# PSUM banks of attention and of the streams beside it: one shared pool of four, or three and one

## The chip, the core and the metric

The kernel runs on one core of a Trainium2 chip. The time is the device time of one execution in microseconds (us), here the median of three runs; beside it stands one execution that the hardware profiler recorded, from which all lines of the profile come. The engines are named as the profile names them: PE is TensorE (its matrix products; PEld its weight loads), DVE is VectorE, ACT is ScalarE, POOL is GpSimd, SP is SyncE, which issues most DMAs. TensorE writes its results into PSUM, which this kernel uses as eight banks of 128 partitions by 512 fp32 numbers.

## What is computed

One decoder block on 2048 tokens of width 1024, in fp32. A modulation of the conditioning vector gives shifts, scales and gates. Then, cut to what matters here:

```
h    = RMSNorm(x) * (1 + scale) + shift
proj = h W_in  ->  q_a, k_a, v_a | q_m, k_m, v_m, o_m, i_m, f_m | g_a, g_m
y_a  = sliding-window attention of rope(q_a), rope(k_a), v_a:  8 query heads, 2 key/value heads,
       16 blocks of 128 queries against 256 keys, a learned sink per head in the softmax
y_m  = chunkwise mLSTM of silu(conv4(q_m, k_m)), v_m and the gates i_m, f_m, with a layer norm
       per head and an output gate
mix  = (sigmoid(g_a) (y_a W_A) + sigmoid(g_m) (y_m W_B)) W_out
x    = x + gate * RMSNorm(mix);   then the same sandwich around a SwiGLU FFN of width 2816
```

## The kernel before

**Stages.** The 2048 tokens are worked in two superblocks of 1024, each of two blocks of 512 (four tiles of 128 tokens). `superblock` gives the order for one of them: queries and keys/values of the first block, `attend(b0)`, mLSTM values of that block, keys/values and queries of the second block, the first quarter of its mLSTM values, `attend(b1)`, the rest of them, then fourteen pairs of wide feature tiles (mLSTM queries, keys, output gate, branch gates), and at last the branch products and `W_out` of both blocks. The FFN follows for both superblocks. A large product is split into a high and a low fp32r part of each operand, so it is three products in PSUM (`mm3`); its sums stand in the four banks of the pool `ps_acc` (tile name `acc`), its split weights in `whi` and `wlo` (L266, L267).

**Small work beside large work.** Attention, gates, rotary steps, h of the next block (`hprep`) and mLSTM are written as generators, "streams". `spawn` registers one, `tick` steps those that are due between the products of the large work, by a planned time `now` that counts TensorE's products; each `yield` gives the planned delay to its next step. So the order in which the code asks for tiles is the order of these planned steps. The final order of instructions on each engine is set when the kernel is built, by a scheduler with a timing model of its own, which can move an instruction ahead of others that wait for a tile or for data.

**The shared banks.** The other four PSUM banks are the pool `ps_mix`. All short users take their bank from it by `mix_tile` (L120), under one tag with four buffers (tile name `mix`):

- `one` in `hprep` (L496): four transposes of x; ScalarE reads the bank twice (L502, L504). Eight such tiles for a block of h.
- `q_stream` (L756) and `k_stream` (L783): transposes of the rotated queries and keys of one token tile (`mix<-ident,tx`), read by ScalarE and VectorE (L763, L764; L789, L790), then stored to `at_d`, from where attention loads them as `at`.
- `gates` (L824): two tiles for a block.
- `attention` (L899): for a block of 128 queries four tiles of scores in two halves (`mix<-at`, read by L927 on ScalarE and L929 on VectorE), after the softmax (L934 to L946, its last step on POOL) two tiles of transposed probabilities (`mix<-ident,tm`, read by L955 and L959), and one of the output (`mix<-tm,at`, read by L968 and L973). Two `attention_stream`s alternate; behind L968 each issues the load of its next block on ScalarE's queue (L896).
- `chunk_state` (L1010) and `chunk_out` (L1051) of mLSTM: seven tiles for a chunk, with `vmt`, `ld` and `cst` as operands.
- `ada_tail` (L404), and in the later stages `h_combine`, `pair_parts` for the FFN and the `Y` sums of `down`.

**Scratch.** `tx` (L123) is a pool of nine tiles of 512 columns in SBUF. `evac_q` (L770) empties a query bank of `acc` into one (L773), and `rope` takes a second; both are held until `q_stream` has stored its result. `evac_kv` (L795, L798) and `k_stream` hold two in the same way. `rope` ends with L752 and L753 on VectorE. In between, `attend(b)` (L998) first finishes the query and key streams of its block, then lets attention go on, and spawns the two attention streams once in a superblock.

Of the kernel before, what the change touches and what calls it, by code (L numbers as in the profile page):

```python
# [10 lines left out]
F32 = mybir.dt.float32  # L11
# [8 lines left out]
P = 128  # L20
# [4 lines left out]
NT = TB // P  # L25
# [47 lines left out]
def decoder_block(ctx: ExitStack, tc: tile.TileContext, a: dict, out: bass.AP, dbg=None):  # L73
# [32 lines left out]
    ps_mix = ctx.enter_context(tc.tile_pool(name="ps_mix", bufs=4, space=PSUM))  # L106
# [6 lines left out]
    def nm(s):  # L113
        uid[0] += 1
        return f"{s}{uid[0]}"

    def acc_tile():
        return ps_acc.tile([P, 512], F32, tag="acc", name=nm("acc"))

    def mix_tile():  # L120
        return ps_mix.tile([P, 512], F32, tag="mix", name=nm("mix"))

    def tx(shape, dtype=F32):  # L123
        return tpool.tile(shape, dtype, tag="tx", name=nm("tx"), bufs=9)
# [1 line left out]
    def tm(shape, dtype=F32):  # L126
        return mpool.tile(shape, dtype, tag="tm", name=nm("tm"), bufs=9)
# [79 lines left out]
    def mm(o, lhsT, rhs, start, stop, resumed=False):  # L207

        n = int(np.prod(rhs.shape[1:]))
        now[0] += max(110.0, n * 0.422) if rhs.dtype == F32R else max(218.0, n * 1.7)  # L210
        T.matmul(o, lhsT=lhsT, rhs=rhs, start=start, stop=stop, skip_group_check=resumed)  # L211

    def transpose(o, i):
        now[0] += 110.0
        k = i.shape[0]
        T.transpose(o, i, ident[:k, :k])  # L216

    def spawn(gen, delay=0.0):
        st = [now[0] + delay, gen, False]
        streams.append(st)  # L220
        return st
# [506 lines left out]
    def superblock(sb):  # L728
# [170 lines left out]
        def attention(n, a_, ahead):  # L899
            first = n == 0  # L900
            b, t = divmod(n, NT)
            k0 = P if first else 0
            ks = slice(k0, 2 * P)
            af = a_.bitcast(F32)
            later = None
            qth, qtl = (a_[:, i * 512:(i + 1) * 512].rearrange("p (j q) -> p j q", j=GQ) for i in range(2))
            kth, ktl = (a_[:, AT_K + 2 * i * P:AT_K + 2 * (i + 1) * P] for i in range(2))
            vat = af[:, AT_V:].rearrange("p (u d) -> p u d", u=2)
            mx = small.tile([P, HQ], F32, tag="mx", name=nm("mx"))
            nm_ = small.tile([P, HQ], F32, tag="nmx", name=nm("nmx"))  # L910
            sums = small.tile([P, HQ], F32, tag="sums", name=nm("sums"))
            es = small.tile([P, HQ], F32, tag="es", name=nm("es"))
            banks = {}
            sc = {g: tm([P, GQ, P]) for g in range(2)}
            for jj in range(2):
                for g in range(2):
                    banks[g, jj] = mix_tile()
                for u in range(2):
                    j = 2 * jj + u
                    for lt, rt, st_, sp_ in ((qth, kth, True, False), (qth, ktl, False, False), (qtl, kth, False, True)):  # L920
                        for g in range(2):
                            pr = slice(g * 64, (g + 1) * 64)
                            mm(banks[g, jj][:, u * 256 + k0:u * 256 + 256], lt[pr, j, :], rt[pr, ks], st_, sp_)
                for g in range(2):
                    bv = banks[g, jj].rearrange("p (u k) -> p u k", u=2)
                    dst = sc[g][:, 2 * jj:2 * jj + 2, :]
                    A.copy(dst, bv[:, :, P:])  # L927
                    mk = m_prev.bitcast(U32).unsqueeze(1).to_broadcast([P, 2, P])
                    V.copy_predicated(dst, mk, negc.unsqueeze(1).to_broadcast([P, 2, P]) if first else bv[:, :, :P])  # L929
                if jj == 0:  # L930
                    yield 0
            for g in range(2):
                hs = slice(g * GQ, (g + 1) * GQ)
                V.tensor_reduce(mx[:, hs], sc[g], axis=AX.X, op=ALU.max)  # L934
            V.tensor_tensor(mx, mx, sinks, op=ALU.max)
            V.tensor_scalar(nm_, mx, -1.0, None, op0=ALU.mult)
            V.tensor_tensor(es, sinks, mx, op=ALU.subtract)
            A.activation(es, es, AF.Exp)
            for g in range(2):
                for j in range(GQ):  # L940
                    hd = g * GQ + j
                    A.activation(sc[g][:, j, :], sc[g][:, j, :], AF.Exp, bias=nm_[:, hd:hd + 1], accum_out=sums[:, hd:hd + 1])
                hs = slice(g * GQ, (g + 1) * GQ)
                V.tensor_tensor(sums[:, hs], sums[:, hs], es[:, hs], op=ALU.add)
                V.reciprocal(sums[:, hs], sums[:, hs])
                G.tensor_tensor(sc[g], sc[g], sums[:, hs].unsqueeze(2).to_broadcast([P, GQ, P]), op=ALU.mult)  # L946
            yield L_SOFT
            pcs, pfs = [], []
            for g in range(2):
                pt = mix_tile()  # L950
                for j in range(GQ):
                    transpose(pt[:, j * P:(j + 1) * P], sc[g][:, j, :])
                pf = tm([P, GQ, P])
                ptv = pt.rearrange("p (j q) -> p j q", j=GQ)
                A.copy(pf, ptv)  # L955
                pfs.append(pf)
                if not first:
                    pc = tm([P, GQ, P])
                    V.scalar_tensor_tensor(pc, cneg.unsqueeze(1).to_broadcast([P, GQ, P]), -1.0, ptv, op0=ALU.is_ge, op1=ALU.mult)  # L959
                    pcs.append(pc)  # L960
                yield L_PT if g == 0 else L_PV
            yps = mix_tile()
            for src_, u, st_, sp_ in ((pfs, int(first), True, first), (pcs, 1, False, True)):
                for g, p_ in enumerate(src_):
                    mm(yps[g * 64:(g + 1) * 64, :], vat[:, u, g * 64:(g + 1) * 64], p_.rearrange("p j q -> p (j q)"), st_, sp_)
            now[0] -= 1500.0
            yh, yl = tm([P, 512], F32R), tm([P, 512], F32R)
            A.copy(yh, yps)  # L968
            y_out = [y_d[b][:, i, :, t * P:(t + 1) * P] for i in range(2)]
            nc.scalar.dma_start(y_out[0], yh.bitcast(F32).rearrange("p (j q) -> p j q", j=GQ))  # L970
            if ahead():
                later = load_at(n + 2, nc.scalar)
            V.tensor_tensor(yl, yps, yh.bitcast(F32), op=ALU.subtract)  # L973
            yield 700.0
            nc.scalar.dma_start(y_out[1], yl.bitcast(F32).rearrange("p (j q) -> p j q", j=GQ))
            return later
# [3 lines left out]
        def attention_stream(u):  # L980
            a_ = None
            for i in range(u, 2 * NT, 2):
                n = b0 * NT + i
                if a_ is None:
                    while i >= ready[0]:
                        yield 1000.0
                    a_ = load_at(n, nc.sync)
                    yield L_LOAD
                    a_ = yield from attention(n, a_, lambda: i + 2 < ready[0])
                else:  # L990
                    yield L_LOAD - 1500.0
                    a_ = yield from attention(n, a_, lambda: i + 2 < ready[0])
                done_att[0] += 1
                yield 500.0

        done_att = [0]

        def attend(b):  # L998
            finish(R["qk"])
            ready[0] = (b - b0 + 1) * NT  # L1000
            if b == b0:
                R["att"] = [spawn(attention_stream(0), L_QK), spawn(attention_stream(1), L_QK + L_ATT2)]
            R["gs", b] = [spawn(gates(b), L_QK)]

# [5 lines left out]
        def chunk_state(c):  # L1010
            b, t = b0 + c // NT, c % NT
# [9 lines left out]
            vc = vmt[n_ % 2]  # L1021
            nc.sync.dma_start(vc[:, :, :MD], vm_d[b][:, t, :].rearrange("p (h d) -> p h d", h=MH))
            yield L_LOAD
            pk = mix_tile()
            for hh in range(MH):
                transpose(pk[:, hh * P:(hh + 1) * P], km[:, hh, :])
            kw = tm([P, MH, P])
# [10 lines left out]
                G.tensor_tensor(qs_, qs_, qm, op=ALU.mult)  # L1038
            R["w", c] = wd, qs_, km, qm, vc
            yield L_KW  # L1040
            pcn = [mix_tile() for _ in range(2)]
            for hh in range(MH):
                mm(pcn[hh // 2][:, (hh % 2) * 129:(hh % 2) * 129 + 129], kw[:, hh, :], vc[:, hh, :], True, True)
            for hh in range(MH):
# [6 lines left out]
        def chunk_out(c):  # L1051
            b, t = b0 + c // NT, c % NT
# [1 line left out]
            cs = slice(t * P, (t + 1) * P)  # L1054
            n_ = b * NT + t
            wd, qs_, km, qm, vc = R["w", c]
            pS = mix_tile()
            for hh in range(MH):
                mm(pS[:, hh * P:(hh + 1) * P], km[:, hh, :], qm[:, hh, :], True, True)
            V.tensor_tensor(wd, pS.rearrange("p (h t) -> p h t", h=MH), wd, op=ALU.mult)  # L1060
# [4 lines left out]
            st = small.tile([P, MH, 6], F32, tag="st", name=nm("st"))  # L1065
            mv = small.tile([P, MH, 2], F32, tag="mv", name=nm("mv"))
            vr = small.tile([P, MH], F32, tag="vr", name=nm("vr"))
            pn = [mix_tile() for _ in range(2)]
            for hh in range(MH):
                o = pn[hh // 2][:, (hh % 2) * 129:(hh % 2) * 129 + 129]  # L1070
                if n_ > 0:
# [20 lines left out]
                o = pn[hh // 2][:, (hh % 2) * 129:(hh % 2) * 129 + P]  # L1092
                A.activation(ym[:, hh, :], o, AF.Identity, scale=cf[:, hh:hh + 1], bias=vr[:, hh:hh + 1])
            yield L_LN
            py = mix_tile()
            for hh in range(MH):
                transpose(py[:, hh * P:(hh + 1) * P], ym[:, hh, :])
            V.tensor_tensor(om, py.rearrange("p (h t) -> p h t", h=MH), om, op=ALU.mult)
# [1019 lines left out]
```

## Time and profile before

| what | value |
|---|---|
| median of 3 runs | 2687.98 us (2685.71 to 2688.53) |
| profiled execution, its own time | 2687.54 us |
| its span, first to last instruction | 2685.5 us |
| mean granted TensorE clock | 0.993 |
| PE busy | 2629.6 us (98%), 12382 products |
| DVE busy | 1988.3 us (74%) |
| ACT busy | 1298.8 us (48%) |
| POOL busy | 140.4 us (5%) |
| DMA moved | 511.89 MB |

Busy time counts an engine's instructions without those that only wait or issue DMAs; products are pipelined, so a busy PE isn't always a PE at its best pitch. In the timelines a row gives the start, the length, the engine, the line of the kernel, the operation, the tiles `out<-in` with their buffer numbers left out, shapes and a count, and in brackets the idle time of that engine just ahead with what ended it. In the windows a row gives a stretch, its length, the busy time of each engine with a count, the granted clock, the DMA engines' share and GB/s.

### The profile page before, as it was taken

What the parts mean: (1) busy time and instruction counts of PE and PEld (TensorE: products, weight loads), DVE (VectorE), ACT (ScalarE), POOL (GpSimd) and SP (SyncE); (2) the same over time, 40 slices, a digit from 0 to 9 for tenths busy, and PEclk for the clock granted to TensorE, in tenths of its full rate; (3) what the DMA queues carried; (4) which work ended last, traced back from release to release, by engine and by line L of the source; (5) the groups of instructions that cost most, each with busy time, mean ns of one, the idle gap of its engine ahead of it and who ended that gap; (6) DMA issues with size and microseconds to landing.
All of it is one profiled execution on the core that took longest, in us unless ns stands there. A gap on an engine that the chain in (4) does not pass through costs nothing.

```text
span 2685.5 us, 35800 instructions
## 1 busy us (share of the span) xinstructions
PE 2629.6 (98%) x12382; PEld 2146.8 (80%) x12382; DVE 1988.3 (74%) x3882; ACT 1298.8 (48%) x2525; POOL 140.4 (5%) x181
## 2 busy tenths in 40 slices
PE   7899999999998999999999999999999999999998
PEld 6777788888886778888877888888777888888886
DVE  7888887768696988876677777775677676666466
ACT  4656544545754654444654343335554333333444
POOL 0100001200101000110000000000000000000000
PEclk9999999999999999999999999999999999999999
DMA  7564456897575644678775555446675232334566
GB/s 252 173 231 144 148 175 185 263 345 246 191 245 160 210 141 151 194 239 321 227 243 176 181 180 180 134 143 219 214 247 188 98 114 97 108 99 148 189 204 219
DMA packets 353637, 511.89 MB, mean 191 GB/s; under 512 B 25120, under 2 KB 213660, under 8 KB 348208
## 3 DMA queue, kind: packets, MB, share of 16 engines
q1 hardware_dynamic: 335240, 493.82, 55.4%
q10 hardware_dynamic: 18216, 15.79, 2.0%
q8 instruction: 97, 1.59, 0.2%
q14 instruction: 84, 0.69, 0.1%
HBM read 357.12 MB, written 144.02 MB: 187 GB/s over the span
## 4 chain that ended last, share of the span: by engine, by line
PE 63%; DVE 3%; DMA 1%; ACT 1%; issue 0%; POOL 0%; SPq 0%; DVEq 0%; POOLq 0%; ACTq 0%
PE acc L211 42%; PE mix L211 20%; DVE hl L1608 1%; PE mix L216 1%; DMA raw<-as_d 1%; ACT hl L1607 1%; DMA raw<-ws_d 0%; DMA raw<-in_w_ffn_down_dram 0%; DVE big L1608 0%; DVE w L1918 0%; DVE big L1931 0%; DVE w L1954 0%; DVE w L1959 0%; ACT big L1653 0%; POOL rs L457 0%
## 5 line engine op out<-in xcount | busy, mean ns | idle before, releaser
L211 PE MATMUL acc<-big,hl 128*128 128x512 f32 x3936 | 933.9, 392 | 1.4 <-ACT hl L1607 0.7
L211 PEld LDWEIGHTS acc<-big,hl 128*128 128x128 f32 x3936 | 732.9, 188 | 164.8 <-issue 10.0
L1607 ACT CAST hl<-raw 128x512 fp32r<-128x512 f32 x732 | 440.7, 621 | 504.7 <-PE acc L211 238.7
L1608 DVE TENSOR_TENSOR hl<-raw,hl 128x512 fp32r<-128x512 f32 x732 | 497.5, 695 | 190.1 <-ACT hl L1607 187.8
L211 PE MATMUL acc<-whi,big 128*128 128x512 f32 (+1 forms) x1216 | 356.7, 374 | 7.9 <-ACT tx L89 3.8
L211 PE MATMUL mix<-big,hl 128*128 128x512 f32 x1056 | 263.0, 390 | 1.7 <-ACT hl L1607 1.0
L211 PEld LDWEIGHTS acc<-whi,big 128*128 128x128 f32 x1216 | 222.1, 191 | 50.9 <-ACT tx L89 4.3
L211 PE MATMUL acc<-hl,hl 128*128 128x512 f32 x1008 | 238.8, 395 | 5.8 <-DVE hl L1608 3.4
L211 PEld LDWEIGHTS mix<-big,hl 128*128 128x128 f32 x1056 | 197.7, 188 | 44.5 <-ACT hl L1607 1.9
L211 PEld LDWEIGHTS acc<-hl,hl 128*128 128x128 f32 x1008 | 188.0, 189 | 52.1 <-DVE hl L1608 8.4
L211 PE MATMUL acc<-wlo,big 128*128 128x512 f32 (+1 forms) x608 | 226.0, 374 | 3.0 <-DVE wlo L267 3.0
L211 PE MATMUL mix<-hl,hl 128*128 128x512 f32 x792 | 182.6, 391 | 1.1 <-DVE hl L1608 0.9
L211 PEld LDWEIGHTS mix<-hl,hl 128*128 128x128 f32 x792 | 147.9, 188 | 34.8 <-DVE hl L1608 3.0
L211 PE MATMUL acc<-big,whi 128*128 128x512 f32 x512 | 158.2, 393 | 0.0
L267 DVE TENSOR_TENSOR wlo<-raw,whi 128x1024 fp32r<-128x1024 f32 (+1 forms) x95 | 109.8, 1156 | 64.6 <-ACT whi L266 58.4
L266 ACT CAST whi<-raw 128x1024 fp32r<-128x1024 f32 (+1 forms) x95 | 93.7, 987 | 112.5 <-PE acc L211 102.5
L211 PEld LDWEIGHTS acc<-wlo,big 128*128 128x128 f32 x608 | 115.6, 190 | 24.0 <-DVE wlo L267 4.6
L457 POOL TENSOR_TENSOR rs<-ms,halves 128x1 f32<-128x1 f32 (+1 forms) x56 | 43.6, 791 | 1647.1 <-DVE ms L455 1637.5
L211 PE MATMUL mix<-hcT4h,hl 128*128 128x512 f32 x352 | 115.6, 389 | 0.7 <-ACT hl L1607 0.7
L211 PE MATMUL acc<-hcT2h,hl 128*128 128x512 f32 x352 | 115.5, 389 | 0.0
L211 PEld LDWEIGHTS acc<-big,whi 128*128 128x128 f32 x512 | 95.4, 188 | 19.6 <-DMA big<-y_d 0.4
L211 PE MATMUL acc<-big,wlo 128*128 128x512 f32 x256 | 97.6, 392 | 0.0
(350 smaller groups left out, 3537.2 us busy)
## 6 DMA issues: line engine op xcount, KB each, us to landing
raw<-in_w_in_dram SPq DMA_DIRECT2D x48, 1024.0 KB, 6.7
as_d<-w SPq DMA_DIRECT2D x154, 256.0 KB, 2.1
raw<-as_d SPq DMA_DIRECT2D x70, 512.0 KB, 3.9
raw<-in_w_ffn_gate_dram SPq DMA_DIRECT2D x22, 1024.0 KB, 5.5
raw<-in_w_ffn_up_dram SPq DMA_DIRECT2D x22, 1024.0 KB, 6.0
raw<-ws_d SPq DMA_DIRECT2D x40, 512.0 KB, 4.6
tx<-in_w_ada_dram SPq DMA_DIRECT2D x64, 256.0 KB, 3.7
g_d<-tx SPq DMA_DIRECT2D x64, 256.0 KB, 2.5
```

The lines of the kernel that those rows point to most:

```text
L211: T.matmul(o, lhsT=lhsT, rhs=rhs, start=start, stop=stop, skip_group_check=resumed)
L216: T.transpose(o, i, ident[:k, :k])
L266: A.copy(hv, src)
L267: V.tensor_tensor(lv, src, hv.bitcast(F32), op=ALU.subtract)
L457: G.tensor_tensor(r[:, :n], ms[:, :n], nhalf[:, :n], op=ALU.pow)
L1607: A.copy(v(hi), src)
L1608: V.tensor_tensor(v(lo), src, v(hi).bitcast(F32), op=ALU.subtract)
```

## The change

The pool's one tag `mix` with four buffers becomes two tags: `mixa` with three and `mixb` with one. The list `attending` is filled in `attend` of a superblock's first block, behind the finish of its query and key streams, and cleared when its eight attention blocks have been stepped through. `att_tile` is always `mixa`. `mix_tile` is `mixb` while `attending` holds something; otherwise it takes `mixa` three times and `mixb` the fourth. `wide_tile` is `mixa` while attention is under way and `mix_tile` otherwise. Attention uses `att_tile`, mLSTM `wide_tile`, all others keep `mix_tile`. No arithmetic and no transfer is changed.

```
+    N_ATT = 3
+    turn, attending = [0], []
+
+    def att_tile():
+        return ps_mix.tile([P, 512], F32, tag="mixa", name=nm("mix"), bufs=N_ATT)
+
     def mix_tile():
-        return ps_mix.tile([P, 512], F32, tag="mix", name=nm("mix"))
+        if not attending:
+            turn[0] += 1
+            if turn[0] % 4 :
+                return att_tile()
+        return ps_mix.tile([P, 512], F32, tag="mixb", name=nm("mix"), bufs=4 - N_ATT)
+
+    def wide_tile():
+        return att_tile() if attending else mix_tile()
...
@@ attention @@
-                    banks[g, jj] = mix_tile()
+                    banks[g, jj] = att_tile()
...
-                pt = mix_tile()
+                pt = att_tile()
...
-            yps = mix_tile()
+            yps = att_tile()
...
                 done_att[0] += 1
+                if done_att[0] == 2 * NT:
+                    attending.clear()
...
             if b == b0:
+                attending.append(b)
...
@@ chunk_state; in the same way pcn, and pS, pn, py of chunk_out @@
-            pk = mix_tile()
+            pk = wide_tile()
```

More of the change, by code (lines that the diff above doesn't have):

```diff
@@ L1040, in chunk_state @@
             yield L_KW
-            pcn = [mix_tile() for _ in range(2)]
+            pcn = [wide_tile() for _ in range(2)]
             for hh in range(MH):
@@ L1056, in chunk_out @@
             wd, qs_, km, qm, vc = R["w", c]
-            pS = mix_tile()
+            pS = wide_tile()
             for hh in range(MH):
@@ L1067, in chunk_out @@
             vr = small.tile([P, MH], F32, tag="vr", name=nm("vr"))
-            pn = [mix_tile() for _ in range(2)]
+            pn = [wide_tile() for _ in range(2)]
             for hh in range(MH):
@@ L1094, in chunk_out @@
             yield L_LN
-            py = mix_tile()
+            py = wide_tile()
             for hh in range(MH):
```

## The prediction

> **What bounds the kernel now.** I read the page first, then the chain that ended last, then the stages in windows, then the timelines of the two weak stages.
>
> ```profile
> PE 2629.6 (98%) x12382; PEld 2146.8 (80%) x12382; DVE 1988.3 (74%) x3882; ACT 1298.8 (48%) x2525; POOL 140.4 (5%) x181
> ...
> PE 63%; DVE 3%; DMA 1%; ACT 1%; issue 0%; POOL 0%; SPq 0%; DVEq 0%; POOLq 0%; ACTq 0%
> ```
>
> ```profile
> 1656.09 5.44 PE acc L211 x24
> ```
>
> TensorE is the bound: 98% busy and nearly all of the chain. Fed without a break it runs 24 wide products in 5.44 us, 227 ns each. No bank layout changes that pitch; a change of banks can only remove or add stretches in which TensorE isn't fed. So I looked for such stretches while attention runs, since outside them the change only renames the same four banks (below). The windows of all engines give two, one for each superblock:
>
> ```profile
> 117.00:132.00 15.00, 10.19 (x50) 6.82 (x49) 11.07 (x29) 12.88 (x42) 4.12 (x4) 0.89 0.26 67
> 794.00:813.00 19.00, 18.71 (x95) 15.73 (x94) 18.39 (x73) 15.19 (x51) 6.07 (x4) 1.00 0.50 162
> ...
> 832.00:857.00 25.00, 17.55 (x74) 9.29 (x73) 13.43 (x38) 14.81 (x52) 4.69 (x5) 0.80 0.38 119
> 857.00:877.00 20.00, 20.00 (x110) 16.54 (x109) 19.13 (x44) 8.49 (x15) 0.00 (x0) 1.00 0.80 265
> ```
>
> The columns are the stretch, its length, busy time of PE, PEld, DVE, ACT, POOL, and then the granted clock. In 832:857 TensorE is idle for 25.00 - 17.55 = 7.45 us and its clock is 0.80; in 117:132 it is idle for 4.81 us at 0.89; right behind, 857:877, nothing is lost. The timeline of PE tells what it ran and waited for in the first:
>
> ```profile
> 831.44 0.97 PE L211 MATMUL mix<-at 64*128 64x256 f32 x6
> 836.68 2.93 PE L211 MATMUL mix<-at 64*128 64x256 f32 x24 [4.26 <-DVE sums L945]
> 841.05 3.31 PE L211 MATMUL mix<-tm,at 128*64 128x512 f32 x8 [0.24 <-ACT tm L955]
> 846.88 1.12 PE L216 MATMUL mix<-ident,tm 128*128 128x128 f32 x4 [2.53 <-POOL tm L946]
> 848.41 1.12 PE L216 MATMUL mix<-ident,tm 128*128 128x128 f32 x4 [0.41 <-POOL tm L946]
> 851.36 0.69 PE L216 MATMUL mix<-ident,tx 128*128 128x128 f32 x2
> 854.72 0.48 PE L211 MATMUL acc<-whi,big 128*128 128x512 f32 x1
> ```
>
> Attention's own waits (4.26 + 0.24 + 2.53 + 0.41 = 7.44 us) are the idle time. They hurt because no projection product (`acc`) runs before 854.72. Why not? The 4.26 us also shows how far planned order and chip differ: the row names DVE L945, but the keys and queries for this block were requested at 828.23, and such a load lands 6.0 to 8.3 us later (836.5 at the latest), so I read it as the load.
>
> ```profile
> 816.46 0.59 ACT L773 COPY tx<-acc 128x512 f32<-128x512 f32 x1 [0.31 <-PE acc L211]
> ...
> 828.23 0.34 ACTq L896 DMA_DIRECT2D at<-at_d  x1
> ...
> 852.25 0.59 ACT L773 COPY tx<-acc 128x512 f32<-128x512 f32 x1
> ```
>
> ```profile
> DMA to landing us min/median/max: 6.0/7.2/8.3
> ```
>
> L773 empties a query bank of `acc` into a `tx` tile. The first of this block is at 816.46, the second at 852.25, just behind the key transposes of 851.36. There are nine `tx` tiles. Each of four `k_stream`s holds two from L798 until its transposes are read, which leaves one: that is the copy at 816.46, whose rotary step wants another. So the query banks stay full, the next projection has no bank, and all hangs on four small key transposes. Their inputs were ready long before:
>
> ```profile
> 802.18 0.23 DVE L753 TENSOR_TENSOR tx<-tx,tx 128x64 f32<-128x64 f32 x1
> ...
> 804.10 0.23 DVE L753 TENSOR_TENSOR tx<-tx,tx 128x64 f32<-128x64 f32 x1
> ...
> 808.17 0.21 DVE L753 TENSOR_TENSOR tx<-tx,tx 128x64 f32<-128x64 f32 x1
> ```
>
> ```profile
> 794.00:813.00 19.00, 0.00 (x0) 0.00 (x0) 0.00 (x0) 0.00 (x0) 1.00 0.50 162
> ```
>
> The last row is the windows view of the tile `mix` alone: from 794 to 813 no engine touches any of the four banks. Keys are rotated at 802 to 808, all banks are still, yet the transposes run at 851. I conclude that `mix` tiles are handed out in the order in which the code asks for them: the keys' tiles were asked for behind those of the first four attention blocks, and attention's next tile waited for its softmax. It isn't a lack of banks but a queue for them.
>
> **The change part by part.**
> (1) Attention gets a queue of its own (`mixa`), and hprep, gates, `k_stream`, `q_stream` and the ada tails another (`mixb`). In superblock 1 the key transposes no longer stand behind softmax and can run near 802 to 809, about 45 us earlier; the `tx` tiles come free before the second query copy is due, and the projection goes on beside attention. What it is worth: idle 7.45 plus (1 - 0.80) x 17.55 = 3.51 of slow clock, 10.96 us at most, 0 at least (attention's waits may still be met by a queue that is in order). The nearest row is 857:877, with the same kinds of work and no loss; I keep 2 us for a load or softmax met too early: **9 us**. Late next is then the softmax itself, with products to run meanwhile.
>
> [...]
>
> (2) In superblock 0 the same queue holds up the second block's h:
>
> ```profile
> 110.44 0.41 PE L216 MATMUL mix<-ident,tm 68*128 68x68 f32 x4
> ...
> 116.52 0.60 PE L216 MATMUL mix<-ident,big 128*128 128x128 f32 x4
> 120.22 1.11 PE L216 MATMUL mix<-ident,tm 128*128 128x128 f32 x4 [3.10 <-POOL tm L946]
> ...
> 127.99 0.66 PE L216 MATMUL mix<-ident,tm 128*128 128x128 f32 x4 [1.19 <-POOL tm L946]
> 128.49 0.60 PE L216 MATMUL mix<-ident,big 128*128 128x128 f32 x4
> ...
> 129.92 0.60 PE L216 MATMUL mix<-ident,big 128*128 128x128 f32 x4
> ```
>
> ```profile
> 119.55 0.77 ACT L502 ACTIVATE big<-mix,sh,s 128x512 fp32r<-128x512 f32 x1
> 120.22 0.76 ACT L504 ACTIVATE big<-mix,sh,s 128x512 f32<-128x512 f32 x1
> ```
>
> `ident,big` are hprep's transposes; those of 128.49 and 129.92 stand right behind attention's waits on POOL. On one bank of their own the last four cost 0.60 + 0.77 + 0.76 = 2.13 us each. After the gates' tile at 110.44 is read (near 113) they would end near 122, or 125 if ScalarE's exponentials come between, against about 132. The keys' projection, which needs them, fills the stall. At most 4.81 + 0.11 x 10.19 = 5.93 us, at least 0; since the gates' tile stays ahead in the same bank, half: **3 us**.
>
> (3) Attention loses a bank. Its two score halves write four tiles in a row. With three, the second half waits for the first to be read:
>
> ```profile
> 838.33 0.65 ACT L927 COPY tm<-mix 128x256 f32<-128x256 f32 x2 [0.59 <-PE mix L211]
> ```
>
> ```profile
> 838.74 0.78 DVE L929 COPY_PREDICATED tm<-m_prev,mix 128x256 f32<-128x256 uint32 x2 [0.58 <-ACT tm L927]
> ```
>
> The copies begin at 838.33 and end at 839.52: 1.2 us for a block, 16 blocks, 19.2 us if TensorE has nothing else, 0 if it has. The row nearest to the usual case has products directly behind the scores:
>
> ```profile
> 889.79 1.69 PE L211 MATMUL mix<-at 64*128 64x256 f32 x24
> 891.41 5.76 PE L211 MATMUL acc<-big,hl 128*128 128x512 f32 x24
> ```
>
> I take **0**, since those products can go between. If that cover is gone, all later products stand behind the waiting half on TensorE, and ScalarE's L927 and the softmax wait for it.
>
> (4) The others share one bank. Only tiles wanted closer together than one is read (2.13 us above) feel it, as the two at 851.36: from the steps of the streams I estimate four such places in a superblock, so 0 to 8 x 1.3 us = 10 us (L763 and L764 or the like read a tile one after the other); products run at those places, so I take 0.
>
> (5) mLSTM's `wide_tile` and the turn in four outside attention. In the windows view of the tile `at`, attention is absent in
>
> ```profile
> 300.00:765.00 465.00, 0.00 (x0) 0.00 (x0) 1.00 0.68 225
> ```
>
> and mLSTM's products run there and beyond:
>
> ```profile
> L211 PE MATMUL mix<-vmt,tm x256: 271/275/277, 399.0 to 1225.4; 128*128 128x129 f32 x128
> ```
>
> No mLSTM step falls into attention, so this part is idle; outside, three tiles in four go to `mixa` and one to `mixb`, a round of four as before: 0. No DMA, no arithmetic and no instruction is added; SP's and POOL's queues keep their work, only earlier for the keys' stores.
>
> **Sum:** 9 + 3 - 0 = 12 us off the profiled execution's 2687.5 (span 2685.5 and 2.0 around it; the median of the runs is 0.4 above): 2675.5, so 2676 against the median.
>
> **Rivals.** *The waits stay.* TensorE's order is fixed at build time, and a load that lands later than planned stops it wherever it stands; if the freed products are placed behind the same waits, only a little of the 12 us comes. For it: the 4.26 us. Against it: 857:877. About 2 us gained, 2686. *Three banks throttle attention.* Price 19.2 us as in (3); it cancels the gain from the tenth uncovered block of 16 on, and with all and the gain it is 2687.5 - 12 + 19.2 = 2694.7. For it: 836.68, where 24 score products run with nothing beside them. Against it: most blocks look like 889.79.
>
> [...]
>
> **How the numbers follow.** A measurement of this kernel tells about 0.2%, 5.4 us, from no change. The forecast, 2667 to 2682, gets 0.62; the waits that stay, 0.18; three banks or the one bank too few, 0.20. From below the range takes the full 10.96 + 5.93, 2670.6, and the 3.78 us of idle TensorE in the stage just before the first weak one, in which the same streams and copies run and which may go or stay:
>
> ```profile
> 760.00:800.00 40.00, 36.22 (x225) 31.20 (x224) 34.73 (x102) 23.15 (x50) 0.00 (x0) 0.96 0.78 260
> ```
>
> That makes 2667. From above it takes the waits that stay and reaches into the slower rival, whose part above 2692 I leave out. Faster 0.62, same 0.18, slower 0.20.
>
> **What would show it.** Right: in superblock 1 key transposes (`mix<-ident,tx`, one each) within some us of L753, no 35 us gap between the first two L773, `acc` products all through the stage of 832:857 and a clock near 1.00 there; in superblock 0 the last hprep transposes before the second softmax wait. Wrong: the gaps on POOL and loads with the same length while the key transposes are early; or score halves with a new 1.2 us gap ended by DVE L929.

## The result, and the profile after

The changed kernel takes 2702.94 us (median of 4 runs, 2701.22 to 2708.84) against 2686.85 us before; the ratio is 1.0065, 95% interval [1.0051, 1.0079]. So it is 0.65% slower, where 0.4% faster was forecast. Its profiled execution took 2702.6 us (span 2700.9, mean clock 0.990), 15.1 us more than that of before.

The page of the changed kernel, part 1 and the head of its chain. The lines of the statements behind L120 are 13 higher than before up to attention (L211 is now L224, L216 is L229), and 16 higher from the mLSTM streams on.

```profile
PE 2639.2 (98%) x12382; PEld 2152.2 (80%) x12382; DVE 1986.1 (74%) x3882; ACT 1299.8 (48%) x2525; POOL 138.5 (5%) x181
...
PE 82%; DVE 8%; DMA 5%; ACT 3%; issue 2%; POOL 0%; SPq 0%; DVEq 0%; POOLq 0%; ACTq 0%
```

The counts of instructions are the same as before; TensorE's busy time is longer, and its mean clock is lower (0.990 against 0.993). To see where, I cut both spans into the same stretches. In each, length minus PE's busy time times the granted clock is what TensorE lost, idle or slow; I call it the **loss**. (The clock is given to two digits, so a loss in 215 us is good to 1 us; a busy PE at clock 1.00 counts as no loss, whatever its pitch.) The windows view of the kernel before (stretch, length, busy PE, PEld, DVE, ACT, POOL, clock, DMA share, GB/s):

```profile
95.00:310.00 215.00, 209.72 (x1082) 158.68 (x1081) 176.84 (x412) 138.61 (x350) 18.65 (x17) 0.99 0.53 173
785.00:820.00 35.00, 34.71 (x202) 29.16 (x200) 30.32 (x101) 21.14 (x63) 6.07 (x4) 1.00 0.51 160
820.00:860.00 40.00, 32.55 (x152) 19.00 (x152) 21.59 (x58) 19.62 (x61) 4.69 (x5) 0.87 0.50 147
785.00:960.00 175.00, 167.26 (x860) 125.02 (x859) 142.34 (x348) 106.89 (x289) 17.59 (x15) 0.97 0.56 181
1300.00:1500.00 200.00, 197.18 (x894) 161.16 (x893) 154.97 (x256) 101.27 (x177) 7.68 (x11) 1.00 0.63 211
```

and of the changed one, with the two windows of the prediction at the end:

```profile
95.00:310.00 215.00, 203.15 (x1025) 152.76 (x1025) 167.59 (x398) 134.59 (x341) 17.89 (x17) 0.95 0.48 160
785.00:820.00 35.00, 27.63 (x193) 24.21 (x193) 29.36 (x82) 22.04 (x68) 2.17 (x3) 0.95 0.63 217
820.00:860.00 40.00, 40.00 (x194) 27.17 (x193) 27.54 (x84) 20.32 (x54) 4.05 (x4) 1.00 0.57 176
785.00:960.00 175.00, 167.57 (x863) 124.50 (x863) 143.02 (x341) 102.88 (x263) 14.01 (x13) 0.99 0.62 200
1300.00:1500.00 200.00, 194.88 (x876) 158.65 (x875) 151.24 (x252) 102.42 (x182) 9.24 (x13) 0.99 0.64 212
...
117.00:132.00 15.00, 9.71 (x34) 6.84 (x34) 10.02 (x36) 12.85 (x44) 4.14 (x4) 0.50 0.01 2
832.00:857.00 25.00, 25.00 (x131) 17.84 (x130) 13.80 (x37) 13.21 (x38) 2.08 (x2) 1.00 0.55 174
```

- **Superblock 1.** 832:857 is full, at clock 1.00: the place that the prediction was built on is mended (820:860: loss 11.7 to 0). But just ahead of it, 785:820, the loss went from 0.3 to 35 - 27.63 x 0.95 = 8.8 us. Over 785:960 it fell only from 12.8 to 9.1, by 3.7 us.
- **Superblock 0.** 117:132, where 3 us were to be gained, has TensorE busy 9.71 us at half clock. Over 95:310 the loss rose from 7.4 to 22.0, by 14.6 us: nearly the whole result.
- **FFN.** 1300:1500 lost 2.8 and loses 7.1 us, 4.3 more.

With 2.5 us less ahead of 95 us (95 - 76.74 x 0.93 = 23.6 before, 95 - 79.41 x 0.93 = 21.1 after), 14.6 - 3.7 + 4.3 - 2.5 = 12.7 of the 15.1 us are placed. In the other stretches the losses differ by under 1.5 us each, some up and some down, and by about nothing in sum; so the last 2.4 us aren't placed, and the two-digit clock can't place them.

The timeline of PE of the changed kernel shows what happens in superblock 0 (rows that waited, one plain h tile, and the last):

```profile
106.17 0.63 PE L229 MATMUL mix<-ident,big 128*128 128x128 f32 x4 [0.90 <-DVE tm L857]
...
112.30 0.75 PE L224 MATMUL acc<-whi,big 128*128 128x264 f32 x4 [1.43 <-DVE big L518]
112.89 0.41 PE L229 MATMUL mix<-ident,tm 68*128 68x68 f32 x4
113.64 0.98 PE L224 MATMUL mix<-at 64*128 64x256 f32 x6 [0.34 <-DVE tm L942]
117.99 1.09 PE L229 MATMUL mix<-ident,big 128*128 128x128 f32 x4 [3.37 <-DVE cl L888]
119.95 0.59 PE L224 MATMUL acc<-whi,big 128*128 128x264 f32 x1 [0.87 <-ACT big L515]
...
121.87 1.05 PE L229 MATMUL mix<-ident,big 128*128 128x128 f32 x4
...
134.90 0.80 PE L229 MATMUL mix<-ident,big 128*128 128x128 f32 x4
```

`ident,big` are h of the second block, `ident,tm 68*128` is the second tile of the gates. Both now live in the single bank, in the order in which they were asked for. The gates' tile is written at 112.89. Its reader, in the timeline of VectorE, comes late:

```profile
117.53 0.32 DVE L888 COPY cl<-mix 128x16 f32<-128x16 f32 x3
```

In the kernel before, the same tile was written at 110.44 and its reader (there L875) came 2.2 us later:

```profile
112.63 0.32 DVE L875 COPY cl<-mix 128x16 f32<-128x16 f32 x3
```

The windows view of the changed kernel shows what VectorE did meanwhile:

```profile
113.00:118.00 5.00, 1.29 (x12) 0.97 (x10) 4.94 (x15) 0.37 (x1) 0.00 (x0) 0.68 0.02 3
```

VectorE is busy for 4.94 of these 5.00 us, nearly all of it with other things, and until L888 is through the next h tile has no bank. TensorE stands 3.37 us at that tile, and no product of `acc` runs between 113.05 and 119.95. And the last h tile is written at 134.90, not near 122: before it was 129.92.

### The profile page after: what moved, and what is told of

The parts are those of the page before. It is cut to its first block, busy times and chain, and to the rows that moved or that the text cites. A ratio compares the mean times of both kernels' runs of the same rounds, so it can differ in the third digit from the quotient of the medians.

```text
span 2700.9 us, 35799 instructions
## 1 busy us (share of the span) xinstructions
PE 2639.2 (98%) x12382; PEld 2152.2 (80%) x12382; DVE 1986.1 (74%) x3882; ACT 1299.8 (48%) x2525; POOL 138.5 (5%) x181
## 4 chain that ended last, share of the span: by engine, by line
PE 82%; DVE 8%; DMA 5%; ACT 3%; issue 2%; POOL 0%; SPq 0%; DVEq 0%; POOLq 0%; ACTq 0%
PE acc L224 58%; PE mix L224 21%; PE mix L229 2%; DVE hl L1624 1%; ACT tm L955 1%; PE acc L89 1%; DMA raw<-in_w_ffn_down_dram 1%; ACT hl L1623 1%; DVE wlo L280 0%; DMA tx<-in_w_ada_dram 0%; DMA raw<-as_d 0%; DMA big<-big 0%; PE mix L89 0%; POOL rs L470 0%; DMA x<-tm 0%
## 5 line engine op out<-in xcount | busy, mean ns | idle before, releaser
L224 PE MATMUL acc<-big,hl 128*128 128x512 f32 x3936 | 933.6, 392 | 2.3 <-ACT hl L1623 1.7
L224 PEld LDWEIGHTS acc<-big,hl 128*128 128x128 f32 x3936 | 732.8, 188 | 164.2 <-issue 7.9
L224 PE MATMUL acc<-whi,big 128*128 128x512 f32 (+1 forms) x1216 | 365.0, 379 | 12.7 <-ACT tx L832 4.1
L224 PEld LDWEIGHTS acc<-whi,big 128*128 128x128 f32 x1216 | 226.3, 195 | 58.6 <-issue 4.9
L224 PE MATMUL mix<-big,hl 128*128 128x512 f32 x1056 | 263.1, 390 | 1.7 <-ACT hl L1623 1.0
L224 PE MATMUL acc<-hl,hl 128*128 128x512 f32 x1008 | 237.3, 393 | 5.4 <-DVE hl L1624 3.4
L224 PE MATMUL acc<-wlo,big 128*128 128x512 f32 (+1 forms) x608 | 229.5, 380 | 4.3 <-DVE wlo L280 3.6
L224 PEld LDWEIGHTS mix<-big,hl 128*128 128x128 f32 x1056 | 197.8, 188 | 44.5 <-DVE hl L1624 1.9
L224 PEld LDWEIGHTS acc<-hl,hl 128*128 128x128 f32 x1008 | 186.8, 188 | 51.2 <-DVE hl L1624 8.8
L224 PE MATMUL mix<-hl,hl 128*128 128x512 f32 x792 | 183.0, 391 | 1.0 <-DVE ms L468 0.9
L224 PEld LDWEIGHTS mix<-hl,hl 128*128 128x128 f32 x792 | 147.8, 188 | 35.3 <-DVE hl L1624 2.2
L224 PE MATMUL acc<-big,whi 128*128 128x512 f32 x512 | 156.9, 392 | 0.0
L224 PEld LDWEIGHTS acc<-wlo,big 128*128 128x128 f32 x608 | 118.4, 195 | 27.4 <-DVE wlo L280 5.6
L224 PE MATMUL acc<-hcT2h,hl 128*128 128x512 f32 x352 | 116.7, 393 | 2.3 <-ACT w L1764 2.3
L224 PE MATMUL mix<-hcT4h,hl 128*128 128x512 f32 x352 | 115.6, 389 | 0.7 <-ACT hl L1623 0.7
L224 PEld LDWEIGHTS acc<-big,whi 128*128 128x128 f32 x512 | 95.5, 188 | 19.3
L224 PE MATMUL acc<-big,wlo 128*128 128x512 f32 x256 | 98.0, 394 | 0.0
```

## The experiments

The theory: the loss of superblock 0 is the single bank, in which the gates and the h of the next block queue up. Rivals: attention is short of banks with three; the fixed turn of four outside attention costs; or the change merely makes the build order everything anew, and the new order is an unlucky one. Each kernel is compared with the kernel before. The losses are worked out as above from each kernel's own windows.

| kernel | ratio to before [95%] | loss 95:310 | loss 785:960 |
|---|---|---|---|
| before | 1 | 7.4 | 12.8 |
| changed | 1.0065 [1.0051, 1.0079] | 22.0 | 9.1 |
| e1_sb1_only | 1.0045 [1.003, 1.006] | 10.6 | 14.5 |
| e2_sb0_only | 1.0063 [1.0046, 1.008] | 19.0 | 9.3 |
| e3_turn_only | 1.0027 [1.0015, 1.0039] | 10.3 | 14.6 |
| e4_two_two | 1.0004 [0.9995, 1.0013] | 2.5 | 8.4 |
| f1_h_wide | 1.0024 [1.0014, 1.0035] | 13.2 | 10.8 |
| f2_gates_wide | 0.9993 [0.9983, 1.0003] | 5.7 | 4.9 |
| f3_h_gates_wide | 1.0036 [1.0023, 1.005] | 16.7 | 1.4 |
| f7_phase | 1.0052 [1.0035, 1.0068] | 10.5 | 18.7 |
| g1_after_phase | 1.0013 [1.0002, 1.0023] | 18.2 | 7.0 |
| g2_turn_phase1 | 1.0038 [1.0027, 1.0048] | 6.7 | 18.4 |
| g3_before_shift | 0.9995 [0.9983, 1.0006] | 7.3 | 14.2 |
| g4_scan_late | 1.0027 [1.0016, 1.0038] | 10.9 | 9.9 |
| g5_gates_phase | 1.0014 [1.0002, 1.0025] | 10.6 | 9.4 |
| h5_pool_both | 1.0065 [1.0049, 1.0082] | 21.4 | 15.7 |
| h6_pool_gates | 1.0013 [1.0004, 1.0023] | 13.7 | 11.7 |
| h8_pool_control | 1.0035 [1.0023, 1.0046] | 10.9 | 16.5 |
| h4_pool_sb1 | 1.0013 [1.0, 1.0026] | 7.4 | 10.2 |
| h10_sb1_gates | 1.0005 [0.9996, 1.0015] | 7.6 | 10.9 |

### One superblock at a time, none, and two banks each

**e1_sb1_only, e2_sb0_only, e3_turn_only**: the split in superblock 1 alone, in superblock 0 alone (the last condition reads `sb == 0`), or nowhere (the line is left out); elsewhere attention takes its tiles in the turn of four as all others do.

```diff
     def att_tile():
-        return ps_mix.tile([P, 512], F32, tag="mixa", name=nm("mix"), bufs=N_ATT)
+        return mixa() if attending else mix_tile()
...
-                attending.append(b)
+                if sb == 1:
+                    attending.append(b)
```

> The split into three banks and one acts in superblock 1 alone; in superblock 0 all users take the four banks in turn. Theory (the one bank beside attention costs in superblock 0, where the gates and the h of the second block share it; in superblock 1 the split is about even, -1.7 us in the traces): 2684 to 2690 us, the 16 us gone. Rival, three banks throttle attention: half of the loss stays, about 2695. Rival, the turn of four costs outside attention: the loss stays, 2697 or more.

> The split acts in superblock 0 alone. Theory (one bank in superblock 0): nearly the whole loss, 13 to 18 us over the kernel before, 2700 to 2705. Rival, three banks throttle attention: half, about 2695. Rival, the turn of four: as the run without any split, 2697 or more, and no more than that.

> No split at all: two tags, and every user takes three banks of one and the fourth in turn through the whole kernel. Theory: no more than the 5 us that the trace of the changed kernel showed ahead of superblock 1's attention, 2685 to 2692. Rival, the turn of four in place of any free bank is the cost: 2697 or more.

Measured: medians of 2697.87, 2702.70 and 2694.07 us. The split in superblock 0 alone is as slow as the whole change, as the theory wanted, and its PE timeline has the same wait at the same tile (its lines stand 3 higher):

```profile
119.70 1.09 PE L232 MATMUL mix<-ident,big 128*128 128x128 f32 x4 [2.70 <-DVE cl L891]
```

But e1 was to be near 2687 and is 11 us slower than before, and e3, with no split at all, 7 us. The theory alone doesn't give these; the rival of the turn, or that of the order, has a part in it.

**e4_two_two**: two banks for attention, two for the others.

```diff
-    N_ATT = 3
+    N_ATT = 2
...
-            if turn[0] % 4 :
+            if turn[0] % 2:
```

> Two banks for attention and two for the others. Theory (the one bank is short, attention's banks are not): better than three and one, 2687 to 2697. Rival, three banks throttle attention: with two, each block's second score half and its output wait too, worse than three and one, 2705 to 2725.

Measured: 2687.18 us, as before. That **three banks throttle attention is out** as the cause of the loss: with two the kernel takes no longer than before. With a second bank for the others the loss of 95:310 is the lowest of all:

```profile
95.00:310.00 215.00, 212.51 (x1074) 162.34 (x1073) 176.93 (x406) 132.95 (x314) 13.68 (x13) 1.00 0.52 172
```

The time doesn't fall with it. Attention's work ends later there, some of it behind 310, and 960:1050 loses 3.0 us where it lost none (PE 86.99 of 90.00 us, clock 1.00). Where the rest goes is left open.

### Who holds the single bank

**f1_h_wide, f2_gates_wide, f3_h_gates_wide**: the changed kernel, with h, the gates' two tiles, or both moved to attention's three banks (the first line is in `one` of `hprep`, the others in `gates`).

```diff
-            ps = mix_tile()
+            ps = wide_tile()
...
-            pg = mix_tile()
+            pg = wide_tile()
...
-            pc_ = mix_tile()
+            pc_ = wide_tile()
```

> As the changed kernel, but the h of the next block takes its tiles from attention's three banks, so the single bank carries gates, keys and queries only. Theory (in superblock 0 the single bank is short because eight h tiles and two gate tiles follow one another in it): most of the 9 us of superblock 0's split come back, 2693 to 2697. Rival, it is the gates' two tiles that hold the bank: 2700 to 2704. Rival, attention's three banks were already short: worse than the changed kernel, above 2706.

> As the changed kernel, but the gates take attention's three banks and h stays in the single bank. Theory (h and gates behind one another): a smaller part comes back, the 3.5 us at the gates' second tile at most, 2698 to 2702. Rival, the gates' tiles are what holds the bank: 2693 to 2696.

> As the changed kernel, with h and gates both in attention's three banks; the single bank has keys and queries alone. Theory (the crowded single bank): about the time of the split in superblock 1 alone or better, 2690 to 2697. Rival, attention's three banks are short: above 2703. Rival, the cost is only in how the build orders the work and not in any bank: anywhere between 2686 and 2706, with no tie to which users share.

Measured: 2692.23, 2684.20 and 2695.79 us. f1 lies just under its theory's band, f2 below both of its bands: moving the two tiles of the gates takes away the whole 0.65% in this order of the build, and I had expected h to matter more. It is one slow reader among quick ones that does the harm, not the number of tiles. In f2's PE timeline the wait for L888 is 0.38 us and falls on attention's scores; in the windows view the clock stays at 1.00 in the stretch that had 0.50:

```profile
108.29 0.47 PE L224 MATMUL mix<-at 64*128 64x256 f32 x2 [0.38 <-DVE cl L888]
...
115.80 0.63 PE L229 MATMUL mix<-ident,tm 128*128 128x128 f32 x4 [2.27 <-DVE tm L942]
```

```profile
117.00:132.00 15.00, 12.35 (x68) 7.46 (x67) 11.85 (x25) 12.26 (x33) 2.08 (x2) 1.00 0.36 115
```

f3 lies inside its theory's band and yet is slower than f1 and f2: with h in attention's banks as well, 95:310 loses 16.7 beside f2's 5.7 us. Whether there the gates' slow reader holds up attention's queue isn't shown.

**g4_scan_late**: the bank stays as it is, the gates only ask for their second tile later, behind the h tiles.

```diff
-L_GATE, L_SCAN = 1800.0, 5500.0
+L_GATE, L_SCAN = 1800.0, 16000.0
```

> The changed kernel, in which the gates ask for their second tile 10.5 us later, behind the h of the next block; every user keeps its bank. Theory (the gates' second tile, which waits for VectorE's scans, holds up the h tiles that queue behind it in the single bank): most of the gain of moving the gates out comes back, 2684 to 2692. Rival, what the gates cost is the bank's time and not their place in its queue: 2699 to 2705.

Measured: 2692.74 us, 1.0027, just above the theory's band; the loss of 95:310 halves, from 22.0 to 10.9, and the wait for L888 is gone from the PE timeline (the h tile at the same place waits for the h tile ahead of it):

```profile
121.73 1.11 PE L229 MATMUL mix<-ident,big 128*128 128x128 f32 x4 [1.54 <-ACT big L517]
```

So in superblock 0 it is the gates' **place in the queue**, and not their use of a bank, that cost the most. (This is one order of the build; the next section shows that the total of a single order says little, the stage more.)

### How much is the order of the build

**f7_phase, g2_turn_phase1**: e3 (no split) with the turn begun two places and one place further on. **g1_after_phase**: the changed kernel, two places on. **g5_gates_phase**: f2, two places on. **g3_before_shift**: the kernel before, any free bank of four, with one planned delay changed (the last two lines).

```diff
-    turn, attending = [0], []
+    turn, attending = [2], []
...
-L_ROPE, L_ROPEK, L_QK, L_ATT2 = 5000.0, 2100.0, 1500.0, 3500.0
+L_ROPE, L_ROPEK, L_QK, L_ATT2 = 5000.0, 2100.0, 1500.0, 3900.0
```

> As the kernel with the turn of four and no split, with the turn begun two places further on: the same banks, the same users, another pairing of tile and bank. Theory (the cost goes with bank pressure): within 3 us of it, 2691 to 2697. Rival, a neutral reshuffle of the built order moves the time by as much as the split does: 5 us or more away from 2694, either side.

> The turn of four without a split, begun one place further on: a third draw of the same banks and users. Theory (giving up any free bank for a fixed turn costs by itself): slower than before again, 2692 to 2703. Rival, it is the built order, which may come out either way: 2682 to 2690.

> The changed kernel with its turn outside attention begun two places further on; the split is the same. Theory (the gates in the single bank are the cost, wherever the turn stands): it stays slow, 2698 to 2708. Rival, the sum of the waits is a matter of the built order: it leaves that band, 2685 to 2696.

> As the changed kernel with the gates in attention's three banks, with the turn begun two places further on. Theory (the gates held up the single bank): stalls of the stage 95 to 140 stay near 11 us and the time within 2682 to 2691. Rival, the 18 us of the first phase were luck of the built order: 2692 or more, with the stage at 15 us or above.

> The kernel before, one tag and any free bank of four, with the second attention stream planned 0.4 us later: another built order with nothing changed in the banks. Theory (the fixed turn and the crowded bank cost, the built order alone doesn't): within 3 us of before, 2683 to 2689. Rival, every other built order costs 7 us or more, and the kernel before sits at a low point: 2692 to 2703.

Measured: 2701.53, 2697.52, 2690.11, 2692.50 and 2684.17 us. (f7's profiled execution was, at 2696.0, the quickest of its runs; the others took 2701 to 2702.) This speaks against me twice. Three draws of the same banks without a split give +0.27%, +0.52% and +0.38%; and **the changed kernel itself, with its turn shifted, is only 0.13% slower than before**, outside the band that the theory gave it. The gain of f2 is gone too: g5 has 1.0014 beside g1's 1.0013, so in this order moving the gates gains nothing in the total, though 95:310 loses 10.6 beside 18.2 us. (g5's time is in the rival's band; over 95:140 it loses 9.4 us, beside 5.5 in f2 and 18.3 in the changed kernel.) What does hold in every draw is the stage. Split in superblock 0 with the gates ahead of h in the single bank, 95:310 loses 18.2 to 22.0 us in all four kernels (changed, e2, g1, h5); without a split there, 6.7 to 10.9 in all nine. The kernels that keep the split but take gates or h out of the bank, or ask for the gates' second tile behind h (f1, f2, f3, g4, g5, h6), lose 5.7 to 16.7. g1's row:

```profile
95.00:310.00 215.00, 205.04 (x1030) 155.58 (x1029) 165.47 (x397) 132.63 (x339) 16.30 (x16) 0.96 0.49 163
```

By the means, 20.2 against 8.7, the split costs superblock 0 some 11 us in the orders tried; the other stages add or take several microseconds by an order that no one chose. That the whole change costs 0.65% is therefore in part a matter of its order.

### The split without the turn

**h5_pool_both**: the pool is closed and opened anew at both ends of attention, so that outside it any of four banks is free again. **h8_pool_control**: the same without a split. **h6_pool_gates**: h5 with the gates in attention's banks.

```diff
+    def open_mix():
+        if ps_mix[1] is not None:
+            ps_mix[1].close()
+        ...
+        ps_mix[0] = ps_mix[1].enter_context(tc.tile_pool(..., bufs=4, space=PSUM))
...
     def mix_tile():
         if not attending:
-            turn[0] += 1
-            if turn[0] % 4 :
-                return att_tile()
+            return ps_mix[0].tile([P, 512], F32, tag="mix", name=nm("mix"))
...
                 attending.append(b)
+                open_mix()
...
                     attending.clear()
+                    open_mix()
```

> The split of three and one while attention is under way, but outside it any free bank of four again: the pool is closed and opened anew at both ends of attention. Theory (the turn costs about 10 us on average, the single bank 7 to 8 in superblock 0, and the freed keys give some back in superblock 1): 2684 to 2692. Rival, the turn is innocent and the single bank is the whole loss: 2697 to 2704. Rival, opening the pool anew costs by itself: as high, but then the control without a split is high too.

> The kernel before with the pool closed and opened anew at the same places and no split. Theory: as before, 2683 to 2690. Rival, the new pool waits until the old one is empty and costs by itself: above 2692.

> As the split without the turn, and the gates take attention's three banks. Theory (neither the turn nor the crowded bank is left, only the freed keys): faster than before, 2672 to 2681. Rival, what is gained by the freed keys is lost again to waits at other places of the built order: 2683 to 2690.

Measured: 2705.55, 2696.47 and 2690.36 us. h5 is as slow as the changed kernel without any turn, so **the turn isn't needed for the loss**, against what I had forecast. Its windows and its PE timeline (lines 11 higher) repeat the changed kernel's superblock 0:

```profile
95.00:310.00 215.00, 203.79 (x1029) 152.95 (x1029) 167.69 (x399) 135.26 (x341) 17.89 (x17) 0.95 0.48 161
```

```profile
118.44 1.09 PE L240 MATMUL mix<-ident,big 128*128 128x128 f32 x4 [3.25 <-DVE cl L899]
```

The control is not free either (1.0035): opening the pool anew is itself one more order, with 8.5 us of loss in 785:820, so of h5's whole time only the part in superblock 0 is read, and whether the turn adds in the changed kernel what the new pool adds here isn't shown. Against h5, taking the gates out (h6) gives back 21.4 - 13.7 = 7.7 us of loss there; its time, forecast at 2672 to 2681, lies just above the rival's band and not below before.

### What becomes of the keys' 10 us

**h4_pool_sb1**: h5 with the split in superblock 1 alone. **h10_sb1_gates**: h4 with the gates in attention's banks.

```diff
-                    attending.append(b)
-                    open_mix()
+                    if sb == 1:
+                        attending.append(b)
+                        open_mix()
```

> The split acts in superblock 1 alone, by a new pool there, and everything else has any free bank of four. Theory (superblock 0's single bank was the loss; in superblock 1 the stall of the stage 820 to 860 falls by 10 us, of which waits elsewhere in the superblock take most): 2682 to 2690, stalls up by some us at 785 to 820 or 860 to 960. Rival, the keys' 10 us are kept once the turn and superblock 0 are left alone: 2674 to 2680.

> As the split in superblock 1 alone by a new pool, with the gates in attention's three banks. Theory (the 10 us are lost to the built order's other waits, not to the gates): within 4 us of that run, 2680 to 2690. Rival, the gates in the single bank take what the keys give: 2674 to 2680.

Measured: 2689.34 and 2688.66 us, both in the theory's band. In h4 superblock 0 is as before, the stage 820:860 is full, and yet nothing is gained:

```profile
785.00:820.00 35.00, 32.67 (x152) 24.46 (x151) 28.27 (x104) 18.68 (x61) 4.16 (x4) 0.83 0.41 126
820.00:860.00 40.00, 40.00 (x207) 30.23 (x205) 26.08 (x67) 22.11 (x64) 4.16 (x4) 1.00 0.63 197
860.00:960.00 100.00, 97.23 (x470) 70.38 (x469) 81.32 (x171) 61.94 (x151) 7.91 (x7) 1.00 0.60 187
```

```profile
800.31 0.98 PE L240 MATMUL mix<-ident,tm 128*128 128x128 f32 x4 [2.33 <-POOL tm L970]
```

The 11.7 us of 820:860 are gone, but 785:820 now loses 7.9 and 860:960 2.8. The row shows what it is at 800: attention's probabilities are transposed before POOL has them ready, the same kind of wait that stood at 846 before; the clock of 0.83 is the larger part of the 7.9. Moving the gates changes nothing here. All thirteen kernels with a split in superblock 1 lose at most 1.6 us in 820:860, the seven without 5.5 to 12.0; over the whole of 785:960 the means are 9.5 and 14.9. About 5 of the 10 us stay, on average over orders; a single order keeps between none and all.

No version beat the kernel before: f2 at 0.9993 [0.9983, 1.0003] can't be told from it.

## Why the prediction was wrong

**Step (4), the others share one bank, failed.** It took 0 of a range of 0 to 10 us, because "products run at those places". They do stand there, but behind the waiting tile: no product of `acc` runs between 113.05 and 119.95, and the one at 119.95 has waited 0.87 us more for ScalarE's read of that tile (L515). The 8 x 1.3 us were priced with readers of 2.13 us; the gates' tile is held for some 4.95 us (from 112.89 until VectorE's last L888 ends, near 117.84). And the price left out the clock, which the prediction had counted for the stalls that it removed: 118 to 133 runs at half clock. Measured, superblock 0 loses 18.2 to 22.0 us with the step against 6.7 to 10.9 without; in the changed kernel the 14.6 us more in this one superblock are beyond the step's upper end for both.

Taking one user, the gates, out of the single bank gives back 7.7 us of loss in superblock 0 (h6 against h5). The prediction saw no lack of banks because all four lay still for 19 us. That was another stage: that four banks idle at 800 us says nothing about one bank at 115.

**Step (2), 3 us from an earlier h, has the wrong sign.** It named the gates' tile "ahead in the same bank" and halved the gain for it. It expected that tile to be read near 113; it was read at 117.53. What the change did was to take h out of attention's queue and put it into the gates'.

**Step (1) was right in its mechanism and wrong in what it is worth.** The keys' transposes came off softmax's queue, and the stage of 832:857 is full. In the PE timeline of the changed kernel they run at

```profile
819.26 0.27 PE L229 MATMUL mix<-ident,tx 128*128 128x128 f32 x1
829.97 0.27 PE L229 MATMUL mix<-ident,tx 128*128 128x128 f32 x1
833.96 0.27 PE L229 MATMUL mix<-ident,tx 128*128 128x128 f32 x1
839.86 0.27 PE L229 MATMUL mix<-ident,tx 128*128 128x128 f32 x1
```

later than the forecast 802 to 809, earlier than 851. But the allowance of 2 us for "a load or softmax met too early" measured 8.8 - 0.3 = 8.5 us in the changed kernel (785:820) and 7.9 - 0.3 + 2.8 = 10.4 in h4. In g1, the same split in another order, it is 4.0 - 0.3 = 3.7. (In windows of 0.2 us, 832:857 of the kernel before has 10.2 us at a clock of 0.50: 3.4, at 836.5 to 839.9, begin at the end of the wait of 4.26 us; the other 6.8, at 846.8 to 853.6, begin at the end of that of 2.53.) In the changed kernel two waits make most of the 8.5, in the views of PE and of ACT's line L548:

```profile
797.89 0.59 PE L224 MATMUL acc<-whi,big 128*128 128x264 f32 x1 [4.09 <-ACT tx L832]
...
815.13 0.50 PE L224 MATMUL acc<-whi,big 128*128 128x512 f32 x1 [2.29 <-ACT tx L811]
```

```profile
L548 ACT CAST big<-big x8: 614/633/654, 794.4 to 800.3; 128x512 fp32r<-128x512 f32 x8
...
its engine sat idle before it (us, times) until:
  DMA big<-big: 4.1, 1
```

ScalarE stood 4.1 us at a cast whose DMA (the sums of h, L548) hadn't landed, and the copies that empty `acc` (L832) stood behind it. The rival "the waits stay" had this right as to kind: 820:860 lost 11.7 us less, and 785:820 8.5 more, so most of the waits moved. It had them as the old waits in the old place, which they are not.

**Step (3), attention on three banks, 0: right.** In the stretch of superblock 0 shown above it is the wait of 0.34 us for L942 at 113.64, and with two banks (e4) the time is that of before. The rival built on it would have given a time in the measured direction for a reason that is false.

**Step (5), the turn outside attention, 0: open.** Its three draws are slower than before by 7 to 14 us, but h5 is as slow without it, and the control h8, without turn or split but with the pool opened anew, loses 0.35%. No run separates a cost of the turn from that of a new order.

**The FFN's 4.3 us** were in no step. The profile has ScalarE wait there for a store before it writes `w`:

```profile
1423.98 0.59 ACT L1764 COPY w<-acc 128x512 f32<-128x512 f32 x1 [5.01 <-DMA x<-tm]
```

In g1, with the same split, the copy at that place waits for nothing and the stage loses 2.8 us, as before; e1 and f2, with a split too, also lose 2.8. So the split alone doesn't bring this part. Why the store is late in one order and not in the other wasn't tried.

**The range** had no term for the new order as such. Kernels with the same bank resources as before (g3, h8, and the turn's three draws) lie from 0.05% below to 0.52% above it, some 15 us, which is more than any single step was given (9 us at most).

## What to carry to other kernels

A bank of one's own takes a user out of one queue and puts it into another: before splitting a pool, list for each part who asks in which order and how long each holds its tile *on the busiest engine that reads it*, because here a slow reader held up all behind it (the gates' tile was held 4.95 us, where an h tile was priced at 2.13). Work that the built order has behind a wait doesn't cover it: in the 3.37 us ahead of 117.99 TensorE ran nothing. And where a build reorders everything, price a change by the stage in which it acts and over several draws with the same resources; one pair of totals tells a 10 us effect from a 10 us reshuffle badly.

## What the runs showed of the hardware

Beside the waits stands a slow clock. In the changed kernel it is 0.50 from 118 to 133, with TensorE busy for 10.70 of these 15.00 us. The windows and the pitch of 264-column products ahead of the slow stretch (0.12 us) and in it (0.22 us):

```profile
118.00:133.00 15.00, 10.70 (x39) 7.58 (x39) 10.02 (x32) 12.94 (x44) 4.14 (x4) 0.50 0.01 1
133.00:140.00 7.00, 7.00 (x44) 6.02 (x43) 2.17 (x5) 3.62 (x6) 0.00 (x0) 0.84 0.31 65
```

```profile
109.01 0.28 PE L224 MATMUL acc<-wlo,big 128*128 128x264 f32 x1
109.13 0.29 PE L224 MATMUL acc<-whi,big 128*128 128x264 f32 x1
...
121.21 0.42 PE L224 MATMUL acc<-wlo,big 128*128 128x264 f32 x1
121.43 0.42 PE L224 MATMUL acc<-whi,big 128*128 128x264 f32 x1
```

In these 15 us TensorE is idle for 4.30 and loses another 5.35 to the clock. But the clock fell early in the wait of 3.37 us, which had begun at 114.62: in windows of 0.2 us it is 1.00 up to 114.8, 0.57 in 114.8:115.0 and 0.50 from there to 135.2. Ahead of that stand the waits of 1.43 and 0.34 us. g4, in which the wait for L888 is gone, has the same two (1.42 and 0.15), and it too is slow behind them: six score products take 1.48 us at 115.80, where six took 0.97 at 112.07, and the 264-column products have a pitch of 0.22 us from 117.59 to 118.92 and again from 124.09 to 125.42. So the wait for the gates' tile isn't what brought the clock down; what did isn't shown. What that wait did to the clock's return isn't shown either: the clock is back at 135.3 in the changed kernel (0.73 in 135.2:135.4, then 1.00), and g4's products still have the slow pitch at 125.42. In f2, where the longest of the waits in 100:126 is 2.27 us, the clock is 1.00 in all windows of 95:140.

In 95:140 the slow clock lasted 3.4 us in the kernel before (windows of 0.1 us: 0.69 in 119.7:119.8, 0.50 up to 123.1, 0.75 in 123.1:123.2) and 20.5 in the changed kernel (114.8 to 135.3). For g4 the mean of 0.89 over these 45 us gives about 9.9, an estimate that takes its clock to be 1.00 or 0.50, as in the other two. In 118:133 of the changed kernel TensorE was busy for 71% of the time, in pieces, and the clock stayed at 0.50.
